# A hybrid encoder layer on one NeuronCore: first chunk pair of the feed-forward as plain products, operands in long-lived slots, second product's first loads moved

## The chip, the cores and the metric

The kernel runs on one core of one Trainium2 chip. The core has TensorE (matmuls into the accumulation memory, PSUM), VectorE, ScalarE and GpSimd (elementwise work on the on-chip memory, SBUF), and SyncE, whose queue issues the DMA transfers here. The engines run side by side, each through its own instructions in order, and wait for each other by semaphores. The metric is the device time of one execution in microseconds, as the median of several runs.

## The reference

One layer: two groups of attention heads side by side, a projection, and a gated feed-forward with a three-tap convolution along the tokens. There are 1024 tokens (and 16 learned meta tokens in front of them, which the output leaves out), 1024 model columns and 2816 hidden columns. Everything is float32.

```python
u = rmsnorm(h, norm_mix_pre)
o_na = rmsnorm(neighbourhood_attention(q_na, k_na, v_na, rpb), na_gain)   # 8 heads
o_gl = gla_bidirectional(q_gl, k_gl, v_gl, g_gl, z_gl, ...)               # 4 heads
mix = jnp.concatenate([o_na, o_gl], axis=-1) @ w_o
h = h + rmsnorm(mix, norm_mix_post)
a = rmsnorm(h, norm_ffn_pre) @ w_ffn_in
ap = jnp.pad(a, ((0, 0), (half, half), (0, 0)))
a = sum(ap[:, j:j + L] * conv_w[j] for j in range(CONV_W)) + conv_b
val, gate = a[..., :D_FF], a[..., D_FF:]
y = (jax.nn.gelu(gate, approximate=True) * val) @ w_ffn_out
return h + rmsnorm(y, norm_ffn_post)
```

## The kernel before

**Precision.** TensorE multiplies in a rounded float32 form (`fp32r`). To keep float32's accuracy each operand is split in two: ScalarE casts it to the rounded form (`hi`), VectorE subtracts that from the original (`lo`). A product of two operands is then three matmuls, hi x hi, hi x lo and lo x hi. So every operand costs one ScalarE and one VectorE pass before TensorE can use it.

**Upstream.** Projections, gated linear attention (GLA) and the meta tokens' part come first, then neighbourhood attention (NA), whose V windows are copied from DRAM to DRAM in layouts of their own (`vw_d`). The projection `W_o` is loaded in 8 blocks (`wor`), split into `woh` and `wol`, and applied to nine token units of 128 (`wo`, units 0 to 8; unit 8 is the last). Each unit then has two norms: `rsa` after `W_o`, and `rsb` ahead of the feed-forward. Of each norm the last step, a product of one column (L147), runs on GpSimd. The normed unit (`un`) is transposed by TensorE (`pt`, L836) and copied into `u2r`, the feed-forward's input with all 1024 tokens. Units 1 to 5 go by way of DRAM (`ut`). The lists `T2` and `T3` write out by hand in which order these steps are put into the program (`wg`: matmuls of a unit, `wn` and `wt`: its norms and transposes, `ul`: a unit read back, `u15`: one column copied, `fr`: the first weight loads).

**First product.** The hidden columns are worked off in 22 chunk pairs j, each of a value and a gate block of 128 columns. Tokens are taken in two halves, the 1024 input columns in two halves as well, so a pair is a product of 2 x 2 blocks, which the kernel does by seven block products in place of eight (`prod`, operations 1 to 7, the Strassen-Winograd scheme). It needs sums of the blocks: of the inputs `a11`, `a12`, `a21`, `a22` once (`a_sum`, VectorE, `as`), of the weights in each pair (`bt`, GpSimd, L920 to L923, from the raw weights `fr`), and of the results (`evac`, `c`) in each pair. The letters `q_r`, `q_x`, `q_z` are PSUM tiles of these products. One block product is 24 matmuls of 128x258 (2 token quarters, 4 blocks of 128 input columns, 3 terms), so a pair has 168. The convolution (`conv`: one ScalarE and two VectorE steps), the GELU and the gating give `y`, stored to `y_d`.

**Second product.** It is a seven-product scheme too, over pairs of chunk pairs. Its operands are y and the output weights themselves, sums of y (`s_sums`, GpSimd, to `s_d`) and sums of the weights (`t_sums`, GpSimd, from loads `w`, to `t_d`). The sums are made during the first product and go through DRAM. Then seven sweeps of 11 steps follow (`sweep`, `operands`): a step loads two raw operands (`ra`, `rb`), splits them, and does 12 matmuls of 128x512, 924 in all (L1111 to L1113). At the end each of 8 token units is finished by its norm and the residual (`hr`, loaded ahead).

**What sets the order.** A scheduler orders each engine's instructions when the program is built, from the order in which the code is written, some priorities, and the tiles' dependences. Tiles come from pools; a pool with n buffers under a tag hands them out in turn, and whoever takes one waits until its last user is done. On the SyncE queue a DMA that waits holds up the ones behind it. Before, the sums of the weights (`t_sums`) stand in even pairs and have a buffer `w` of their own, and the second product's pools open after the first product's have been closed.

## Time and profile before

| | us |
|---|---|
| runs of the kernel before | 1361.99, 1364.66, 1368.95 (median 1364.66) |
| profiled execution: its own time | 1369.85 |
| profiled execution: span of its instructions | 1368.1 |
| TensorE busy (matmuls) | 1266.1 (93%) |
| VectorE, ScalarE, GpSimd busy | 891.3 (65%), 620.8 (45%), 429.3 (31%) |
| DMA | 203.73 MB, 149 GB/s on average |

A row of the trace names an engine (PE is TensorE, PEld its weight loads, DVE VectorE, ACT ScalarE, POOL GpSimd, SP SyncE, SPq its DMA queue), the line of the kernel, the operation, and its tiles with the output before the arrow. Busy shares are averages over stages with different limits, so the trace is read by stretches. A waiting instruction is listed with what released it. Spans on GpSimd are rough.

### The profile page before, as it was taken

What the parts mean: (1) busy time and instruction counts of PE and PEld (TensorE: products, weight loads), DVE (VectorE), ACT (ScalarE), POOL (GpSimd) and SP (SyncE); (2) the same over time, 40 slices, a digit from 0 to 9 for tenths busy, and PEclk for the clock granted to TensorE, in tenths of its full rate; (3) what the DMA queues carried; (4) which work ended last, traced back from release to release, by engine and by line L of the source; (5) the groups of instructions that cost most, each with busy time, mean ns of one, the idle gap of its engine ahead of it and who ended that gap; (6) DMA issues with size and microseconds to landing.
All of it is one profiled execution on the core that took longest, in us unless ns stands there. A gap on an engine that the chain in (4) does not pass through costs nothing.

```text
span 1368.1 us, 23454 instructions
## 1 busy us (share of the span) xinstructions
PE 1266.1 (93%) x9024; PEld 1136.5 (83%) x9026; DVE 891.3 (65%) x1444; ACT 620.8 (45%) x1182; POOL 429.3 (31%) x402
## 2 busy tenths in 40 slices
PE   7979999999899899996799898999999985999997
PEld 6869888889778668775799898999999974888776
DVE  5481365455354657668898988878878853455557
ACT  5443544523244555555444343544444432445543
POOL 1170001000122326433667778555454311000001
PEclk9989999999999899997899999999999997999999
DMA  6311132112875974443256556332322218767734
GB/s 201 117 38 48 39 90 82 58 56 67 262 227 171 283 225 147 156 169 124 97 196 211 188 204 240 113 109 94 123 93 96 76 65 294 272 193 217 236 108 169
DMA packets 116432, 203.73 MB, mean 149 GB/s; under 512 B 17376, under 2 KB 50496, under 8 KB 116320
## 3 DMA queue, kind: packets, MB, share of 16 engines
q1 hardware_dynamic: 116320, 202.23, 44.6%
q8 instruction: 71, 1.16, 0.3%
q14 instruction: 41, 0.34, 0.1%
HBM read 145.64 MB, written 66.19 MB: 155 GB/s over the span
## 4 chain that ended last, share of the span: by engine, by line
PE 67%; DMA 12%; POOL 7%; DVE 6%; issue 4%; ACT 2%; SPq 1%; POOLq 0%; DVEq 0%; ACTq 0%
PE q_r L967 4%; PE q_r L968 4%; PE q_r L969 4%; PE r L1111 3%; PE r L1112 3%; PE r L1113 3%; DMA w<-in_w_ffn_out_dram 2%; PE pna L178 2%; DMA ra<-y_d 2%; PE pna L179 2%; PE pna L180 2%; PE q_z L968 2%; PE q_z L967 2%; PE q_z L969 2%; PE ops L690 2%
## 5 line engine op out<-in xcount | busy, mean ns | idle before, releaser
L967 PE MATMUL q_r<-ah,bh 128*128 128x258 f32 x704 | 202.7, 288 | 23.2 <-ACT c L1015 16.1
L968 PE MATMUL q_r<-al,bh 128*128 128x258 f32 x704 | 201.5, 286 | 1.0 <-DVE al L152 1.0
L969 PE MATMUL q_r<-ah,bl 128*128 128x258 f32 x704 | 198.7, 286 | 0.0
L967 PEld LDWEIGHTS q_r<-ah,bh 128*128 128x128 f32 x704 | 135.8, 193 | 25.5 <-ACT c L1015 17.1
L968 PEld LDWEIGHTS q_r<-al,bh 128*128 128x128 f32 x704 | 135.9, 193 | 1.3 <-DVE al L152 1.3
L969 PEld LDWEIGHTS q_r<-ah,bl 128*128 128x128 f32 x704 | 135.1, 193 | 0.0
L152 DVE TENSOR_TENSOR bl<-rb,bh 128x512 fp32r<-128x512 f32 x77 | 53.0, 690 | 79.1 <-ACT bh L151 73.0
L967 PE MATMUL q_z<-ah,bh 128*128 128x258 f32 x352 | 100.6, 286 | 3.3 <-DVE c L1065 3.2
L968 PE MATMUL q_z<-al,bh 128*128 128x258 f32 x352 | 100.4, 285 | 0.0
L969 PE MATMUL q_z<-ah,bl 128*128 128x258 f32 x352 | 99.9, 284 | 0.0
L908 DVE TENSOR_TENSOR bl<-bt,bh 128x512 fp32r<-128x512 f32 x88 | 85.0, 966 | 5.5 <-ACT bh L906 5.5
L151 ACT CAST bh<-rb 128x512 fp32r<-128x512 f32 x77 | 47.7, 622 | 87.4 <-PE r L1112 33.1
L1010 ACT ACTIVATE g<-g 128x512 f32<-128x512 f32 x44 | 27.8, 633 | 130.8 <-DVE g L1003 130.8
L920 POOL TENSOR_TENSOR bt<-fr,fr 128x512 f32<-128x512 f32 x22 | 47.7, 2167 | 117.9 <-DVE bl L908 54.7
L908 DVE TENSOR_TENSOR bl<-fr,bh 128x512 fp32r<-128x512 f32 x66 | 63.9, 970 | 24.3 <-ACT bh L906 24.1
L147 POOL TENSOR_TENSOR rsc_r<-rsc_v,nhalf 128x1 f32<-128x1 f32 x8 | 5.7, 715 | 222.2 <-DVE rsc_v L146 222.2
L1111 PE MATMUL r<-bh,ah 128*128 128x512 f32 x176 | 55.7, 396 | 20.4 <-ACT bh L151 20.4
L967 PEld LDWEIGHTS q_z<-ah,bh 128*128 128x128 f32 x352 | 67.2, 191 | 4.2 <-DVE c L1065 4.2
L1112 PE MATMUL r<-bh,al 128*128 128x512 f32 x176 | 68.3, 395 | 0.0
L1113 PE MATMUL r<-bl,ah 128*128 128x512 f32 x176 | 68.2, 395 | 0.0
L969 PEld LDWEIGHTS q_z<-ah,bl 128*128 128x128 f32 x352 | 67.3, 191 | 0.0
L968 PEld LDWEIGHTS q_z<-al,bh 128*128 128x128 f32 x352 | 67.1, 191 | 0.0
(355 smaller groups left out, 4011.4 us busy)
## 6 DMA issues: line engine op xcount, KB each, us to landing
fr<-in_w_ffn_in_dram SPq DMA_DIRECT2D x44, 512.0 KB
...
```

Of the source, the lines that this page charges most:

```text
L151: nc.scalar.copy(hi, src)
L152: nc.vector.tensor_tensor(lo, src, hi.bitcast(F32), ALU.subtract)
L178: mm(ps[:m, :n], wh, uh[:, k, t0 : t0 + n], start=(k == 0), stop=False)
L908: nc.vector.tensor_tensor(lo, src, hi.bitcast(F32), ALU.subtract)
L920: nc.gpsimd.tensor_sub(f[5], b12, b11)
L967: mm(ps[:, t, :258], hi[:, k, :], ah[:, k, c], start=(first and k == 0), stop=False, skip_group_check=True)
L968: mm(ps[:, t, :258], hi[:, k, :], al[:, k, c], start=False, stop=False, skip_group_check=True)
L969: mm(ps[:, t, :258], lo[:, k, :], ah[:, k, c], start=False, stop=(k == 3), skip_group_check=True)
L1010: nc.scalar.activation(g, g, AF.Gelu_apprx_tanh)
L1111: mm(ps, A[0][:, tk], B[0], start=first, stop=False, skip_group_check=True)
L1112: mm(ps, A[1][:, tk], B[0], start=False, stop=False, skip_group_check=True)
L1113: mm(ps, A[0][:, tk], B[1], start=False, stop=last, skip_group_check=True)
```

## The change

- **Input.** `u2r` becomes two tiles `u2a` and `u2b` of 514 columns, one for each token half with its overlap; the overlapping columns are copied by GpSimd. The copies out of PSUM move to ScalarE, except one of unit 8. Units 3 to 5 are read back into buffers of the weight ring `fr`, and `T3` has another order.
- **Pair 0.** It is done by eight plain block products (`plain_prods`), first both of the first token half, then those of the second, the last of them after unit 8's transposes. Its results are convolved in quarters (128x256). It needs no weight sums (`prep`), no result sums, and takes its PSUM from the pools of the stage before. Pairs 1 to 21 keep the seven products.
- **Operands.** The split inputs live in slots of two pools that stay open to the end: `mixp` ("m", where the GLA output was) and `wop` ("w0" to "w7", where the split `W_o` blocks were). Splits and sums of the inputs are made in two column parts. The pools release buffers tile by tile (`reuse_waits="tile"`).
- **Weight sums.** `t_sums` moves to odd pairs, ahead of `s_sums`, and its tiles share the ring "y" of 6 buffers with the gated outputs. Stores go by halves.
- **Second product.** The raw operands of the first sweep's first eight steps (`pre`) are loaded in the last pair into "m", "w4" and "w5". The raw ring has 6 buffers for both operands (before 8 + 8), the split ring 9 (before 3 of each kind), the splits of operation 4 lie in "m", "w0" to "w7" and 4 more buffers, the residual ring has 4 buffers (before 5), and the PSUM banks are assigned by number.

The first place is SyncE's queue while the last attention heads begin. `vw_d` are the copies of V windows, `wor` the raw `W_o` blocks, `kt` and `vt` operands of attention. Before:

```order
L553 DMA vt_0_2_4795<-vw_d_0_2_147 96x3x256
L727 DMA wor_5044<-in_w_o_dram 128x1024
L203 DMA v_d<-pvn_s_4751 128x256
L727 DMA wor_5050<-in_w_o_dram 128x1024
L553 DMA vt_0_3_4797<-vw_d_0_3_148 72x3x256
L849 DMA g_norm_mix_post<-in_norm_mix_post_dram 128x1024
L635 DMA kt_0_2_5099<-kT_d_58 128x576
L635 DMA kt_0_2_5101<-kT_d_59 128x576
L502 DMA vw_d_1_0_141<-v_d 264x1x256
```

After:

```order
L202 DMA v_d<-pvn_s_4751 128x256
L554 DMA vt_0_3_4797<-vw_d_0_3_148 72x3x256
L503 DMA vw_d_1_0_141<-v_d 264x1x256
L503 DMA vw_d_1_1_142<-v_d 352x1x256
L503 DMA vw_d_1_2_143<-v_d 352x1x256
L503 DMA vw_d_1_3_144<-v_d 264x1x256
L503 DMA vw_d_1_0_149<-v_d 192x1x256
L503 DMA vw_d_1_1_150<-v_d 256x1x256
L503 DMA vw_d_1_2_151<-v_d 256x1x256
L503 DMA vw_d_1_3_152<-v_d 192x1x256
L731 DMA wor_5044<-in_w_o_dram 128x1024
L731 DMA wor_5049<-in_w_o_dram 128x1024
```

The two `W_o` loads stood ahead of the window copies and now stand behind all eight.

The second place is the seam before the first product, on two engines. First TensorE, between the last `W_o` products (`wo`) and the first product of the feed-forward. `pt_7` and `pt_8` are transposes of units 7 and 8, `c_...` the plain products of pair 0, `q_r` a product of the seven. Before:

```order
L836 MATMUL pt_7_0_7032<-ident,un_7_6774 128x128 x4
L836 MATMUL pt_7_1_7038<-ident,un_7_6774 128x128 x4
L836 MATMUL pt_5_0_7046<-ident,ut_7044 128x128 x4
L836 MATMUL pt_5_1_7052<-ident,ut_7044 128x128 x4
L836 MATMUL pt_8_0_7099<-ident,un_8_6916 128x128 x4
L836 MATMUL pt_8_1_7105<-ident,un_8_6916 128x128 x4
L967 MATMUL q_r<-ah_7117,bh_1_7062 128x258
L967 MATMUL q_r<-ah_7117,bh_1_7192 128x258
L967 MATMUL q_x<-ah_7119,bh_2_7074 128x258
```

After:

```order
L764 MATMUL wo_1_1_7002<-wo_5081,mh_1_6982 128x512
L842 MATMUL pt_7_0_7061<-ident,un_7_6766 128x128 x4
L963 MATMUL c_0_7084<-a_7073,bh_11_7045 128x258
L964 MATMUL c_0_7084<-a_7073,bh_11_7045 128x258
L842 MATMUL pt_7_1_7067<-ident,un_7_6766 128x128 x4
L965 MATMUL c_0_7084<-a_7073,bl_11_7047 128x258
...
L965 MATMUL c_0_7217<-ah_7186,bl_22_7059 128x258
L842 MATMUL pt_8_0_7242<-ident,un_8_6908 128x128 x4
L842 MATMUL pt_8_1_7248<-ident,un_8_6908 128x128 x4
...
L965 MATMUL c_1_7283<-ah_7186,bl_22_7059 128x258
L963 MATMUL q_r<-a_7073,bh_1_7313 128x258
L964 MATMUL q_r<-a_7073,bh_1_7313 128x258
```

The first product no longer comes behind unit 8's transposes; the products of three of pair 0's four token quarters stand ahead of unit 8's, and pair 1 follows.

At the same place, GpSimd. `bt` are weight sums of a pair, `rsa_r` and `rsb_r` the last steps of the units' norms, the last of them those of unit 8. Before:

```order
L920 TENSOR_TENSOR bt_5_7196<-fr_1_7190,fr_0_7188 128x512
L921 TENSOR_TENSOR bt_6_7197<-fr_1_7190,bt_5_7196 128x512
L922 TENSOR_TENSOR bt_7_7198<-fr_1_7190 128x512
L810 TENSOR_TENSOR un_8_6916<-un_8_6916,g_norm_mix_post 128x512
L923 TENSOR_TENSOR bt_4_7199<-fr_0_7188,bt_6_7197 128x512
L147 TENSOR_TENSOR rsb_r<-rsb_v,nhalf 128x1
L147 TENSOR_TENSOR rsa_r<-rsa_v,nhalf 128x1
L147 TENSOR_TENSOR rsb_r<-rsb_v,nhalf 128x1
```

After:

```order
L938 TENSOR_TENSOR bt_5_7317<-fr_1_7311,fr_0_7309 128x512
L939 TENSOR_TENSOR bt_6_7318<-fr_1_7311,bt_5_7317 128x512
L940 TENSOR_TENSOR bt_7_7319<-fr_1_7311 128x512
L815 TENSOR_TENSOR un_8_6908<-un_8_6908,g_norm_mix_post 128x512
L941 TENSOR_TENSOR bt_4_7320<-fr_0_7309,bt_6_7318 128x512
L146 TENSOR_TENSOR rsa_r<-rsa_v,nhalf 128x1
L938 TENSOR_TENSOR bt_5_7580<-fr_1_7574,fr_0_7572 128x512
L939 TENSOR_TENSOR bt_6_7581<-fr_1_7574,bt_5_7580 128x512
L940 TENSOR_TENSOR bt_7_7582<-fr_1_7574 128x512
L146 TENSOR_TENSOR rsb_r<-rsb_v,nhalf 128x1
L941 TENSOR_TENSOR bt_4_7583<-fr_0_7572,bt_6_7581 128x512
```

Unit 8's `rsb_r` still stands behind the sums of two pairs; these are pairs 1 and 2, where they were 0 and 1.

The third place is SyncE's queue at the end of the first product. `ra`, `rb` and `r` are raw operands of the second. Before:

```order
L1040 DMA y_d_81<-y_12165 128x2x512
L1040 DMA y_d_82<-y_12414 128x2x512
L1040 DMA s_d_103<-y_12165 128x2x512
L1040 DMA s_d_104<-y_12414 128x2x512
L1100 DMA ra_0_12586<-y_d_61 128x512
L1100 DMA rb_0_12588<-in_w_ffn_out_dram 128x512
L1100 DMA ra_1_12610<-y_d_63 128x512
L1100 DMA rb_1_12612<-in_w_ffn_out_dram 128x512
```

After:

```order
L1119 DMA pre_12487<-y_d_61 128x512
L1120 DMA pre_12487<-in_w_ffn_out_dram 128x512
...
L1105 DMA y_d_81<-y_12248 128x512 x2
L1092 DMA t_d_115<-w_0_12657 128x2x512
L1092 DMA t_d_115<-w_1_12658 128x2x512
L1105 DMA y_d_82<-y_12508 128x512
L1105 DMA s_d_104<-y_12508 128x512
L1105 DMA y_d_82<-y_12508 128x512
L1105 DMA s_d_103<-y_12248 128x512 x2
L1105 DMA s_d_104<-y_12508 128x512
L1181 DMA r_8_12852<-y_d_77 128x512
L1181 DMA r_8_12852<-in_w_ffn_out_dram 128x512
```

The first eight steps' loads have gone ahead of the last pair's stores, and what stands behind these now is the ninth step's load, `r_8`.

The diff, cut to what the text speaks of:

```diff
 T3 = (
-    "wt 6", "wn 7", "u15", "ul 1", "ul 2", "wg 8", "ul 4", "wn 8", "ul 3", "wt 7", "ul 5", "fr",
+    "wt 6", "wn 7", "ul 1", "ul 2", "wg 8", "ul 3", "ul 4", "ul 5", "u15", "wn 8", "fr", "wt 7",
 )
...
+    wop = ctx.enter_context(tc.tile_pool(name="wop", reuse_waits="tile", bufs=1))
...
+    def quad(n, name, dt=F32R):
+        return wop.tile([P, 4, HC], dt, tag=f"w{n}", name=name)
...
-        raw = pp3.tile([P, D], F32, tag="xr", name=f"wor{k}", bufs=2)
+        raw = pp3.tile([P, D], F32, tag="ut", name=f"wor{k}", bufs=2)
...
+        plain = j == 0
...
+        if plain:
+            for op, b in (("11", b11), ("21", b21), ("12", b12), ("22", b22)):
+                b_split(j, op, b)
+            return
...
+    parts = (slice(0, 258), slice(258, HC))
...
+    def prods(ps, w, A, t, first, last):
+        c = slice(256 * t, 256 * t + 258)
+        for k in range(4):
+            mm(ps, w[0][:, k, :], A[0][:, k, c], start=(first and k == 0), stop=False, skip_group_check=True)
+            mm(ps, w[0][:, k, :], A[1][:, k, c], start=False, stop=False, skip_group_check=True)
+            mm(ps, w[1][:, k, :], A[0][:, k, c], start=False, stop=(last and k == 3), skip_group_check=True)
...
+    def plain_prods(half, t):
+        for c, bank in (("1", (ps_b, ps_a)), ("2", (ps_c, ps_s))):
+            ps = plain[half, c, t] = bank[half == 0](f"c{half}{c}_{t}")
+            for x, op in enumerate((1, 2) if half == 0 else (0, 4)):
+                prods(ps[:, :258], wts[0, f"{x + 1}{c}"], aops[op], t, x == 0, x == 1)
...
+    for t in range(2):
+        plain_prods(0, t)
...
+    plain_prods(1, 0)
     step2("wt 8")
+    a_split(0, a21, parts[1])
+    a_split(4, a22, parts[1])
+    plain_prods(1, 1)
...
+    prep(1)
...
+    def ring4(name):
+        return fc.tile([P, 4, 256], F32, tag="y", name=name, bufs=6)
...
-        w = fc.tile([P, 2, 2, 512], F32, tag="w", name=f"w{k}")
+        w = [ring4(f"w{k}_{c}").rearrange("p (h d) b -> p h (d b)", h=2) for c in range(2)]
...
+        if j == NFC - 1:
+            t = mixp.tile([P, 8, HC], F32, tag="m", name="pre1")
+            raws = [t[:, x, :512] for x in range(8)]
+            for w in (4, 5):
+                t = quad(w, f"pre{w}", F32)
+                raws += [t[:, x, :512] for x in range(4)]
+            for k in range(8):
+                pre.append(raws[2 * k : 2 * k + 2])
+                nc.sync.dma_start(pre[k][0], y_d[2 * k][0])
+                nc.sync.dma_start(pre[k][1], a["w_ffn_out"][2 * k][0])
...
         if j % 2:
+            t_sums(j // 2)
             s_sums(j // 2, ys[j - 1], y)
-        else:
-            t_sums(j // 2)
...
-            raws[x] = half(f"r{x}", f"r{x}{op}_{k}", 8)
-            nc.sync.dma_start(raws[x], src)
...
+        if op == 1 and k < len(pre):
+            raws = pre[k]
+        else:
+            raw = (fb if i % 2 else fo).tile([P, KC, P], F32, tag="fr", name=f"r{op}_{k}", bufs=3)
...
-        hrs[i] = fo.tile([P, D], F32, tag="hr", name=f"hr{i}", bufs=5)
+        hrs[i] = fo.tile([P, D], F32, tag="hr", name=f"hr{i}", bufs=4)
```

## Rows read from the trace of the kernel before

**Rows 1.** Stretches (microseconds), busy time and instructions of each engine, clock, DMA.

```profile
core 0: us, PE busy (x) PEld busy (x) DVE busy (x) ACT busy (x) POOL busy (x), PEclk, DMA share, GB/s
460.00:500.00 40.00, 38.48 (x326) 27.37 (x327) 23.26 (x70) 23.96 (x62) 10.73 (x20) 0.92 0.89 269
620.00:640.00 20.00, 11.85 (x58) 8.83 (x56) 16.33 (x25) 9.78 (x17) 9.10 (x8) 0.75 0.57 202
640.00:680.00 40.00, 27.79 (x192) 26.99 (x193) 35.76 (x25) 19.36 (x20) 22.07 (x8) 0.78 0.19 66
700.00:800.00 100.00, 92.68 (x742) 90.90 (x741) 89.26 (x91) 42.69 (x72) 73.98 (x48) 0.98 0.61 211
800.00:900.00 100.00, 93.23 (x750) 92.42 (x749) 83.73 (x90) 42.48 (x73) 66.71 (x43) 0.97 0.47 166
900.00:1000.00 100.00, 100.00 (x837) 100.00 (x837) 83.84 (x101) 47.68 (x80) 50.92 (x31) 1.00 0.31 111
1120.00:1130.00 10.00, 2.80 (x24) 2.58 (x22) 5.00 (x7) 2.68 (x4) 0.00 (x0) 0.74 0.13 52
1145.00:1160.00 15.00, 15.00 (x60) 12.20 (x59) 7.00 (x11) 6.53 (x11) 0.00 (x0) 0.87 1.03 381
1160.00:1280.00 120.00, 120.00 (x530) 98.98 (x529) 63.71 (x99) 59.10 (x108) 0.00 (x0) 1.00 0.72 233
```

**Rows 2.** TensorE's waits, 700 to 1110, then 1110 to 1368: total, times, longest.

```profile
PE q_r L967 <- ACT c L1015: 5.4, 3, 2.6
PE q_r L967 <- DVE y L1003: 5.0, 4, 2.6
...
PE r L1111 <- ACT bh L151: 20.4, 1, 20.4
```

**Rows 3.** Timeline, SyncE's queue and TensorE near 456: start, duration, operation [idle before].

```profile
456.38 9.56 SPq L502 DMA_DIRECT2D vw_d<-v_d  x8
457.59 0.79 PE L757 MATMUL wo<-woh,mh 128*128 128x512 f32 x1 [4.55 <-ACT woh L151]
```

**Rows 4.** Timeline at the first seam: TensorE, then VectorE, then GpSimd.

```profile
622.19 0.40 PE L759 MATMUL wo<-wol,mh 128*128 128x512 f32 x1
640.22 0.80 PE L967 MATMUL q_r<-ah,bh 128*128 128x258 f32 x2 [2.04 <-ACT ah L151]
639.01 2.30 DVE L981 TENSOR_TENSOR as<-u2r 128x2056 f32<-128x2056 f32 x1
661.32 4.50 DVE L152 TENSOR_TENSOR al<-as,ah 128x2056 fp32r<-128x2056 f32 x2
681.12 0.75 DVE L1002 SCALAR_TENSOR_TENSOR g<-c,vec,g 128x512 f32<-128x512 f32 x1 [0.88 <-ACT g L999]
655.32 11.64 POOL L920 TENSOR_TENSOR bt<-fr,fr 128x512 f32<-128x512 f32 x1 [20.54 <-DVE bl L908]
667.03 1.27 POOL L921 TENSOR_TENSOR bt<-fr,bt 128x512 f32<-128x512 f32 x1
```

**Rows 5.** Chain of waits: start, length, what, in three places.

```profile
783.40 6.04 DMA fr<-in_w_ffn_in_dram
...
1143.19 2.04 PE r L1111 x4
...
1292.03 4.33 DMA ra<-y_d
```

**Rows 6.** The page's groups: weight splits beside idle and beside busy GpSimd.

```profile
L152 DVE TENSOR_TENSOR bl<-rb,bh 128x512 fp32r<-128x512 f32 x77 | 53.0, 690 | 79.1 <-ACT bh L151 73.0
...
L908 DVE TENSOR_TENSOR bl<-bt,bh 128x512 fp32r<-128x512 f32 x88 | 85.0, 966 | 5.5 <-ACT bh L906 5.5
```

**Rows 7.** Timeline at the second product's start and end.

```profile
1130.45 1.26 POOL L1032 TENSOR_TENSOR y<-y,y 128x512 f32<-128x512 f32 x1 [27.24 <-issue]
1134.42 1.70 SPq L1040 DMA_DIRECT2D s_d<-y  x2
1360.81 0.39 PE L1113 MATMUL r<-bl,ah 128*128 128x512 f32 x1
```

More of the change, by code (lines that the diff above doesn't have):

```diff
@@ L61 @@
 BTOT = 12 * (24 + 32 + 24)
+HC = 2 * 256 + 2
 NLATE = 5
@@ L756, in wo_mm @@
                 kk = k if part else 4 + k
-                mm(ps, mh[:, k, :], woh[kk][:, cs], start=(k == 0), stop=False)
+                x = mm(ps, mh[:, k, :], woh[kk][:, cs], start=(k == 0), stop=False)
+                if i == 8 and hf == 0 and k == 0:
+                    tc.keep_in_program_order(x)
                 mm(ps, ml[:, k, :], woh[kk][:, cs], start=False, stop=False)
@@ new lines, in gated @@
+    def gated(j, name, src, val):
+        if len(val.shape) == 2:
+            g = mixp.tile([P, 256], F32, tag="ssq", name=f"g{j}_{name}", bufs=2)
+        else:
+            g = mixp.tile([P, 2, 256], F32, tag="mnb", name=f"g{j}_{name}", bufs=4)
+        conv(j, 1, src, g)
+        nc.scalar.activation(g, g, AF.Gelu_apprx_tanh)
+        nc.vector.tensor_mul(val, val, g)
+    y0 = [mixp.tile([P, 2, 256], F32, tag="mnb", name=f"y0_{x}", bufs=4) for x in range(2)]
+    for half in range(2):
+        for t in range(2):
+            val = y0[half][:, t]
+            conv(0, 0, plain[half, "1", t][:, :258], val)
+            gated(0, f"{half}{t}", plain[half, "2", t][:, :258], val)
@@ L954 @@
+    psum_s.close()
     ps1s = ExitStack()
[L955 removed]
+    ps1 = ps1s.enter_context(tc.tile_pool(name="ps1", reuse_waits="tile", bufs=1, space=bass.MemoryType.PSUM))
     acc1 = {}
[L958 to L969 removed]
@@ L989, with acc_tile @@
-    a_split(4, a22)
-    nc.vector.tensor_tensor(s2, a12, s2, ALU.subtract)
-    a_split(3, s2)
+    def acc_tile(j, key):
+        tag = f"r{j % 2}" if key == "r" else key
+        acc1[j, key] = ps1.tile([P, 2, 512], F32, tag=f"q{tag}", name=f"q{j}_{key}")
+    for j, key in ((1, "z"), (2, "r"), (1, "r"), (1, "x")):
+        acc_tile(j, key)
+    def prod(j, op, key, first):
+        if (j, key) not in acc1:
+            acc_tile(j, key)
+        for t in range(2):
+            prods(acc1[j, key][:, t, :258], wts[j, op], aops[op], t, first, True)
@@ new lines, with a_sum @@
+    prod(1, 1, "r", True)
+    prod(1, 2, "x", True)
+    def a_sum(dst, x, y, alu, c):
+        nc.vector.tensor_tensor(dst[:, :, c], x[:, :, c], y[:, :, c], alu)
+    for c in parts:
+        a_sum(a22, a21, a22, ALU.add, c)
+        a_sum(s2, a22, a11, ALU.subtract, c)
+        a_split(6, s2, c)
+    for c in parts:
+        a_split(5, a22, c)
+    for c in parts:
+        a_sum(a21, a11, a21, ALU.subtract, c)
+        a_split(7, a21, c)
+    ops_tiles(3, 6, 7)
+    for c in parts:
+        a_sum(s2, a12, s2, ALU.subtract, c)
+        a_split(3, s2, c)
@@ L1115 @@
     o4 = []
+    steps = []
+    late = []
     def sweep(op, ps, first):
@@ L1123, in sweep, with copies @@
                 o4.append(operands(4, len(o4)))
-    def copies(name, ps):
-        r = [half(name, f"{name}_{t}", 4) for t in range(4)]
+    def copies(dst, ps):
         for t in range(4):
-            nc.scalar.copy(r[t], ps[t])
-        return r
-    R = [ps2.tile([P, H], F32, tag="r", name=f"r{t}", bufs=4) for t in range(4)]
-    Z = [ps2.tile([P, H], F32, tag="z", name=f"z{t}", bufs=4) for t in range(4)]
+            nc.scalar.copy(dst[t], ps[t])
+    banks = [ps2.tile([P, H], F32, name=f"bank{t}") for t in range(8)]
+    R, Z = banks[2:4] + banks[6:], banks[:2] + banks[4:6]
     sweep(1, R, True)
-    c11 = copies("c11", R)
+    c11 = [half("c11", f"c11_{t}", 4) for t in range(4)]
+    copies(c11, R)
     sweep(2, Z, True)
@@ L1140 @@
     sweep(6, R, False)
-    c12 = copies("c12", R)
+    c12 = [half("c12", f"c12_{t}", 4) for t in range(4)]
+    copies(c12, R)
+    c22 = [half("c22", f"c22_{t}", 4) for t in range(4)]
     sweep(7, R, False)
-    c22 = copies("c22", R)
+    copies(c22, R)
+    t = mixp.tile([P, 8, HC], F32R, tag="m", name="late")
+    late += [t[:, x, :512] for x in range(8)]
+    for w in (0, 1, 2, 3, 4, 5, 6, 7):
+        t = quad(w, f"late{w}")
+        late += [t[:, x, :512] for x in range(4)]
+    late += [half("late", f"late{x}", 4, F32R) for x in range(4)]
     sums = fo.tile([P, 2 * 8], F32, name="sums")
```

205 lines of the change are left out of this document (101 added, 104 removed).

## The prediction

> **What bounds the kernel now.** I read the page first, then the table by stretches, then TensorE's waits, then the timelines at the seams. TensorE is busy in most stretches, and every other engine has room on average, so a time is saved only where TensorE stands. In [rows 1] the reader sees where. From 900 to 1000 us TensorE runs 837 matmuls of 258 columns in 100 us without a gap, 0.1195 us each; from 1160 to 1280 it runs 530 of 512 columns in 120 us, 0.2264 each. These two paces price all that follows.
>
> The first feed-forward product has 22 x 168 = 3696 matmuls, 441.7 us at that pace. It begins at 640.22 [rows 4] and its last 24 matmuls end 2.80 us after 1120 [rows 1], so it takes 482.6 us: 40.9 are lost. From 640 to 680 there are 192 matmuls (22.9 us' worth) in 40 us: 17.1 lost. From 700 to 900 there are 742 + 750 = 1492 (178.3) in 200 us: 21.7 lost, to waits for VectorE's and ScalarE's convolutions [rows 2] and a granted clock of 0.98 and 0.97, so that some of it ran at 1.2 GHz. That leaves 2.1. Between the products TensorE stands 20.4 us for the first operand of the second [rows 2]. The second product runs from 1143.19 [rows 5] to 1361.2 [rows 7], 218.0 us, where 924 x 0.2264 = 209.2 are needed. The span ends 6.9 later, at 1368.1. Ahead of it all, TensorE loses 20 - 11.85 = 8.2 us from 620 to 640 [rows 1], when the last token unit's norms are on their way.
>
> **Upstream: W_o loads behind the window copies.** Before, the first W_o loads are issued ahead of eight copies of V windows, whose issue takes 9.56 us, and TensorE still waits 4.55 us for the first weights [rows 3]. After, the copies come first. The copies issue earlier too, since nothing of W_o is ahead of the store they wait for, and TensorE has attention work to put in the gap. So the cost lies between 0 (the earlier issue makes up for all) and 10 (the whole issue time, to the next microsecond); a gain is excluded, since no load moves forward. I take the middle, **+5**. The row shows 269 GB/s from 460 to 500 [rows 1], and the eight copies move 2128 KB, 8.1 us at that rate. The Trainium skill, "DMA: Bandwidth & Descriptors", section "Queues, rings and completion order", says that each DMA engine takes a queue's descriptors in ring order; by that alone the loads would lose those 8.1 us, and the sum would be 3 us longer.
>
> **First seam.** The change lets chunk pair 0 begin on the first token half. Its eight products have 192 matmuls in place of 168: 24 x 0.1195 = +2.9 us of TensorE. In return TensorE has 192 + 48 = 240 matmuls (28.7 us' worth: all of pair 0, and two products of pair 1) to do while VectorE makes the other operands, and VectorE is the bound there. Its order after the last W_o product (622.6, [rows 4]) holds, up to the last operand part that pair 1's third and fourth products need: 20 splits and sums of half width at 1.15 (half of the 2.30 row), 7 weight splits at 0.69 [rows 6], 16 quarter convolutions at about 0.42 and 4 gates at 0.4 (estimates from the 0.75 row of twice the width), and the last unit's own steps, about 5.6 (seven of 0.7 to 1.3, by the same rows). That is 23.0 + 4.8 + 6.7 + 1.6 + 5.6 = 41.7 us: 664.3.
>
> To it come waits. The last unit's second norm runs through GpSimd, and in the new order its small product stands behind the weight sums of pairs 1 and 2. Those of pair 2 want a weight block whose buffer is free only after pair 1's sums: five GpSimd steps of about 1.5, a load of 6.04 [rows 5], three more steps. From about 627, when pair 1's second block can be there (its buffer is free after pair 0's first splits, at about 621, and the load takes 6.04), this gives 627 + 7.5 + 6.0 + 4.5 = 645, against 637.5 at which VectorE (14.7 us of the above) reaches the step that waits: some 8 us. Stretching of VectorE beside GpSimd adds the rest; a weight split takes 966 ns in the first product and 690 in the second, where GpSimd rests [rows 6]. Low end: 664.3 + 8.2, the idle time of 620 to 640, = 672.5. High end: 41.7 x 966/690 = 58.4, plus 8.2, = 689.2. I take **679**, nearer the low end because GpSimd is busy in part of that time only.
>
> **Pacing.** 3720 - 240 = 3480 matmuls remain at 679: 415.9 us, to 1094.9. Before, GpSimd is busy 73.98 and 66.71 of 100 us from 700 to 900, running weight sums ahead, and 50.92 from 900 to 1000, where TensorE never waits [rows 1]. Paced, the 16 GpSimd steps of each two pairs at 50.92/31 = 1.64 take 26.2 of 40.1 us, 65%: near the row of 800 to 900 in load, but without its convolution lag from the seam. I leave 3 us of waits (bounds 0 and 21.7): the first product ends at **1097.9**, 24.9 earlier.
>
> **Second seam.** The first eight steps' operands are loaded during the last pair into slots that are dead by then, so the 20.4 us go. TensorE does not stop, so the slow start goes too: 4 + 60 matmuls took 1160 - 1143.2 = 16.8 us, at a granted clock of 0.87 in the last 15 [rows 1], where 14.5 are needed: 2.3. What is late next is the ninth step's operand, whose load stands in SyncE's queue behind the last sums' stores. Before, these are issued at 1134.42 for 1.70 us, 13.3 after the product's end; with a load of 4.33 [rows 5] and a split it is there at about +19, wanted after 8 x 12 x 0.2264 = 21.7. But GpSimd's four sums took 1.26 each beside an idle VectorE [rows 7]; at 1.74 they end 2 later, and y may be late by as much. I take **+2** (0 to 5). The shallower residual ring ties the last residual loads to earlier finishes: **+1** (0 to 4.33, a load). The shallower raw ring I hold at no cost; the fourth rival is the case in which it costs.
>
> **Sum.** 1097.9 + 5 + (218.0 - 2.3 + 2) + 6.9 + 1 = 1328.5 against the span of 1368.1: -39.6. The profiled execution took 1369.85, 1.75 beyond its span, and is the longest of about the same as the three runs (median 1364.66). Taken from the median: **1325**.
>
> **Rivals.**
> *Gains in full.* Upstream 0, 672.5 at the seam, no waits left, no late operand, no tail: 5 + 6.5 + 3 + 2 + 1 = 17.5 less, 1307.5. For it: each low end has a row. Against: all at once.
>
> *GpSimd starved at the first seam.* One GpSimd sum shows 11.64 us from 655.32, while VectorE runs long two-input operations back to back, where the next, beside little, takes 1.27 [rows 4]. If that happens to the sums ahead of the last unit's norm, VectorE reaches the waiting step and stands for most of the eight steps, some 10 us: 1335. Against: halves of 1.15 leave more openings than the 4.50 pairs of before. The Trainium skill, "SBUF — State Buffer", section "Who interferes with whom", states the rule that speaks against this change: a VectorE operation with two SBUF inputs and a GpSimd operation that reads SBUF exclude each other, and the second to start is blocked. The 11.64 row agrees with it.
>
> *Raw ring too shallow.* Two sweeps issue 33 operand loads in 22 steps of 2.72 us (59.8 us) over six buffers: a buffer must come round within 10.9. With a load of 4.33, the split and the queue at 14 (an estimate), the sweeps take 33 x 14/6 = 77: +17, 1342. Against: 233 GB/s in the steady part leave room [rows 1].
>
> *Seam and pacing gain nothing.* If VectorE (89.26 of 100 us busy from 700) is the bound and the lag merely moves, the 24.9 stay: 1350.
>
> *Slower: GpSimd paces the first product.* The weight sums now share six buffers with the gated outputs, so a late sum stalls the convolutions and then TensorE. With 16 steps in 40.1 us this begins at a mean step of 2.51 us; at 2.78 it eats the whole gain. At 2.9 it costs (46.4 - 40.1) x 10 = 63: 1388. Against: 1.64 in the row of 900 to 1000 and 73.98/48 = 1.54 in that of 700 to 800. For: the 11.64 row.
>
> **Chances.** Forecast 0.44; gains in full 0.12; starved GpSimd 0.15; raw ring 0.12; no gain in seam and pacing 0.10; slower 0.07. The range of 1305 to 1352 leaves out the last and some of the edges. A measurement of this kernel tells about 0.5%, 6.8 us, from no change. Faster by more: all but the slower case and the part (0.05) of the fifth case in which upstream is dear as well and a load is late: 0.87. Within: 0.05. Slower: 0.08.
>
> **What would show it.** The first W_o product some 5 us later than 457.59; pair 0's first matmul before the last unit's transposes, pair 1's third product at about 684 (with upstream); 837 matmuls per 100 us from there on; no wait over 5 us between the products; the second product in about 218 us. A GpSimd row of over 5 us at the first seam, waits for raw operands in the second product, or convolutions that wait for a buffer of stores would prove me wrong, each for its rival.

## The result: 0.6% faster, a fifth of what was forecast

The changed kernel takes 1356.62 us (median of 10 runs, 1352.45 to 1361.46) against 1364.78 (10 runs) of the kernel before: ratio 0.9938, 95% interval 0.9918 to 0.9959. That is faster, by 8 us where 40 were forecast, and the time lies above the range; the interval reaches to both sides of the 0.5% that the prediction set as its bound. The profiled execution took 1360.31 us with a span of 1358.6, 9.5 less than the span before.

The table by stretches of the changed kernel, with the columns of [rows 1]:

```profile
460.00:500.00 40.00, 32.24 (x261) 24.01 (x259) 19.32 (x57) 18.77 (x49) 9.24 (x19) 0.66 0.97 289
620.00:640.00 20.00, 17.67 (x96) 13.99 (x94) 8.90 (x17) 11.28 (x24) 4.04 (x6) 1.00 0.27 96
640.00:660.00 20.00, 18.88 (x136) 17.68 (x137) 17.85 (x19) 14.44 (x26) 11.30 (x8) 1.00 0.43 141
660.00:680.00 20.00, 11.22 (x71) 9.98 (x70) 19.50 (x28) 10.73 (x16) 5.27 (x4) 0.78 0.10 40
680.00:700.00 20.00, 12.51 (x92) 12.04 (x90) 19.22 (x23) 9.09 (x14) 7.88 (x1) 0.84 0.23 70
700.00:800.00 100.00, 97.06 (x788) 96.69 (x788) 84.95 (x89) 42.73 (x72) 63.27 (x40) 0.97 0.40 141
800.00:900.00 100.00, 97.06 (x805) 96.46 (x804) 89.06 (x98) 45.72 (x78) 58.09 (x37) 1.00 0.41 146
900.00:1000.00 100.00, 95.79 (x792) 95.01 (x792) 89.76 (x94) 43.99 (x75) 62.43 (x39) 1.00 0.46 161
...
1160.00:1280.00 120.00, 120.00 (x531) 99.39 (x530) 65.72 (x103) 61.26 (x112) 0.00 (x0) 1.00 0.70 234
```

Read it against [rows 1] in four places. From 460 to 500 TensorE is busy 32.24 in place of 38.48, at a granted clock of 0.66 in place of 0.92. From 660 to 700 VectorE is busy 38.72 of 40 us while TensorE has 23.73. From 700 on no stretch is poor any more, but none is full: 788, 805 and 792 matmuls, where 742, 750 and 837 stood. The second product's pace is as it was.

TensorE's timeline of the changed kernel at four places: the first `W_o` product, the last of the unbroken run of these products, the third and fourth products of chunk pair 1, and the first matmul of the second product (start, duration, operation, idle time before and its releaser). Below it stand two matmuls of the kernel before, which the table needs.

```profile
473.65 0.80 PE L760 MATMUL wo<-wo,mh 128*128 128x512 f32 x1 [5.68 <-ACT wo L150]
...
629.62 0.39 PE L764 MATMUL wo<-wo,mh 128*128 128x512 f32 x1
...
696.11 0.55 PE L963 MATMUL q_z<-ah,bh 128*128 128x258 f32 x1 [5.23 <-DVE y L1012]
...
700.63 0.58 PE L963 MATMUL q_r<-ah,bh 128*128 128x258 f32 x1 [2.89 <-ACT c L1076]
...
1137.81 0.39 PE L1197 MATMUL bank<-oh,oh 128*128 128x512 f32 x1
```
```profile
612.04 0.40 PE L758 MATMUL wo<-woh,ml 128*128 128x512 f32 x1
...
683.64 0.28 PE L968 MATMUL q_z<-al,bh 128*128 128x258 f32 x1
```

The first product ends at 1137.8, the second starts in the same microsecond and ends at 1351.6. The spans split like this. In the last column the upstream term is measured at the `W_o` matmul with 36 of them still to come, 612.04 before and 629.62 after (there the unbroken run ends). The seam is from that one to the matmul with which 3474 of the first product's are left, 683.64 before and 700.63 after: the first one behind the last wait of the seam.

| part | forecast | measured |
|---|---|---|
| upstream, to the end of the `W_o` run | +5 | +17.6 |
| first seam | -4 | -0.6 |
| rest of the first product | -21 | -2.0 |
| between the products | -20.4 | -20.4 |
| second product and tail | +0.7 | -4.1 |
| span | -39.6 | -9.5 |

One of five terms holds to the microsecond. Upstream costs more than three times its 5 us, and of the 25 us that the first seam and the rest of the first product were to give, 2.6 came. The experiments take these three first.

### The profile page after: what moved, and what is told of

Its sections match the earlier page's. It is cut to its first block, busy times and chain, and to the rows that moved or that the text cites. A ratio compares the mean times of both kernels' runs of the same rounds, so it can differ in the third digit from the quotient of the medians.

```text
span 1358.6 us, 23572 instructions
## 1 busy us (share of the span) xinstructions
PE 1272.8 (94%) x9048; PEld 1142.4 (84%) x9050; DVE 910.7 (67%) x1453; ACT 620.3 (46%) x1198; POOL 430.2 (32%) x401
## 4 chain that ended last, share of the span: by engine, by line
PE 66%; DVE 18%; DMA 6%; issue 4%; ACT 4%; SPq 1%; POOL 0%; DVEq 0%; ACTq 0%; POOLq 0%
DVE bl L921 5%; PE bank L1198 4%; PE bank L1197 4%; PE bank L1199 4%; PE q_r L963 3%; PE q_r L964 3%; PE q_r L965 3%; PE ops L691 2%; PE wo L760 2%; PE wo L764 2%; PE wo L763 2%; PE pna L177 2%; PE pna L178 2%; PE pna L179 2%; PE q_z L963 2%
## 5 line engine op out<-in xcount | busy, mean ns | idle before, releaser
L963 PE MATMUL q_r<-ah,bh 128*128 128x258 f32 x504 | 144.3, 286 | 12.4 <-ACT c L1076 12.4
L964 PE MATMUL q_r<-al,bh 128*128 128x258 f32 x504 | 143.3, 284 | 0.0
L965 PE MATMUL q_r<-ah,bl 128*128 128x258 f32 x504 | 143.0, 284 | 0.0
L151 DVE TENSOR_TENSOR ol<-r,oh 128x512 fp32r<-128x512 f32 x116 | 74.5, 687 | 46.9 <-ACT oh L150 46.6
L1197 PE MATMUL bank<-oh,oh 128*128 128x512 f32 x264 | 102.9, 390 | 2.9 <-DVE c L1263 2.9
L1198 PE MATMUL bank<-oh,ol 128*128 128x512 f32 x264 | 102.7, 389 | 0.0
L1199 PE MATMUL bank<-ol,oh 128*128 128x512 f32 x264 | 102.2, 389 | 0.0
L150 ACT CAST oh<-r 128x512 fp32r<-128x512 f32 x116 | 65.6, 619 | 50.3 <-PE bank L1198 40.8
L921 DVE TENSOR_TENSOR bl<-fr,bh 128x512 fp32r<-128x512 f32 x67 | 67.2, 1007 | 17.8 <-ACT bh L919 17.6
L177 PE MATMUL pna<-uh,wna_h 128*128 128x272 f32 (+2 forms) x192 | 64.2, 335 | 4.8 <-DVE qsl L151 4.8
L178 PE MATMUL pna<-ul,wna_h 128*128 128x272 f32 (+2 forms) x192 | 65.0, 339 | 0.0
```

The lines of the kernel that those rows point to most:

```text
L150: nc.scalar.copy(hi, src)
L151: nc.vector.tensor_tensor(lo, src, hi.bitcast(F32), ALU.subtract)
L177: mm(ps[:m, :n], wh, uh[:, k, t0 : t0 + n], start=(k == 0), stop=False)
L178: mm(ps[:m, :n], wh, ul[:, k, t0 : t0 + n], start=False, stop=False)
L921: nc.vector.tensor_tensor(lo, src, hi.bitcast(F32), ALU.subtract)
L963: mm(ps, w[0][:, k, :], A[0][:, k, c], start=(first and k == 0), stop=False, skip_group_check=True)
```

## Upstream: the W_o loads

SyncE's queue (start, time that the issue took, operation), in the kernel before and then in the changed one:

```profile
448.08 0.49 SPq L727 DMA_DIRECT2D wor<-in_w_o_dram  x1
448.66 0.52 SPq L203 DMA_DIRECT2D v_d<-pvn_s  x1
449.54 0.33 SPq L727 DMA_DIRECT2D wor<-in_w_o_dram  x1
```
```profile
451.16 0.58 SPq L202 DMA_DIRECT2D v_d<-pvn_s  x1
...
457.18 7.66 SPq L503 DMA_DIRECT2D vw_d<-v_d  x8
464.88 1.95 SPq L731 DMA_DIRECT2D wor<-in_w_o_dram  x2
```

The copies did not issue earlier than the 456.38 of [rows 3]; the loads issue some 16 us later than before, when two had gone out by 449.54. The granted clock (the first number behind the engines) fell in both kernels; before, from 440 to 480:

```profile
440.00:460.00 20.00, 13.86 (x132) 10.96 (x131) 9.85 (x37) 7.49 (x19) 4.08 (x10) 0.81 0.82 230
460.00:480.00 20.00, 19.56 (x172) 15.39 (x173) 13.33 (x46) 13.06 (x37) 7.14 (x13) 0.85 0.91 294
```

After:

```profile
440.00:460.00 20.00, 18.27 (x210) 15.60 (x209) 11.91 (x51) 9.53 (x29) 5.20 (x11) 0.99 0.61 181
460.00:480.00 20.00, 14.32 (x101) 10.51 (x100) 5.98 (x14) 6.71 (x16) 2.24 (x5) 0.50 0.89 286
```

So part of what 460 to 500 shows had its counterpart before 460 in the kernel before: from 440 to 500 the clock is 0.89 there and 0.77 after. `e1_wo_first` puts the loads ahead of the copies again, by their priority alone.

```diff
-        nc.sync.dma_start(raw, a["w_o"][:, k, :])
+        with tc.high_priority(offset=1000):
+            nc.sync.dma_start(raw, a["w_o"][:, k, :])
```

> The changed kernel with one thing undone: the loads of the raw W_o blocks go ahead of the eight V window copies again. Theory (the upstream term was sized too small): the first W_o product, at 473.6 us in the changed kernel and at 457.6 before the change, comes at about 463, the granted clock from 460 to 500 rises from 0.66 to about 0.9, and the time falls by 10 to 16 us, to about 1343. Rival (the late W_o loads are made up for by attention work that TensorE does meanwhile, and the loss lies at the first seam): the first W_o product moves but the time falls by 4 us at most.

Measured: 1347.37 us, ratio 0.9875 (0.9824 to 0.9925), 9 below the changed kernel. Its first `W_o` product starts at 460.4, its `W_o` run ends at 612.9, and its stretch has the clock and the work of before:

```profile
460.00:500.00 40.00, 38.05 (x308) 27.35 (x309) 25.85 (x73) 25.75 (x64) 9.63 (x20) 0.92 0.97 300
```

So the order of these loads costs about 9 us of median time. With four runs of `e1` this is rough: its interval and that of the changed kernel just touch. It is a little under the theory's 10 to 16 and over the rival's 4. In profiles of kernels that keep the order (`e2`, `e3`, `e4`, `e7`, `e8` below) the `W_o` run ends between 621.4 and 627.0, in `e1`, `e6` and `e10` between 612.9 and 617.7; the 629.6 of the changed kernel is the long end, and the +17.6 of the table holds some of such scatter.

## The first product: the weight sums

Four kernels take the sums apart. `e2_no_wsums` leaves the 44 GpSimd subtractions of the weights out, with their loads and stores kept; the instruction order on TensorE, VectorE and ScalarE is unchanged.

```diff
-        nc.gpsimd.tensor_sub(b11, b12, b11)
-        nc.gpsimd.tensor_sub(b12, b22, b12)
-        nc.gpsimd.tensor_sub(b22, b22, b11)
-        nc.gpsimd.tensor_sub(b21, b21, b22)
```

> The changed kernel without the arithmetic of the second product's weight sums on GpSimd (44 instructions; loads and stores stay, so t_d holds the raw weights and the output is not the layer's). The order on TensorE, VectorE and ScalarE is the same. Theory (GpSimd's sums slow VectorE wherever they stand, so pacing spread the loss and did not remove it): TensorE's waits from 700 to 1110, 14.8 us in the changed kernel, fall under 3, a weight split on VectorE falls from about 1.04 to under 1.0 us, and the time falls by 15 to 20 us, to about 1339. Rival (VectorE's own work in the new order is the bound, GpSimd or not): waits stay over 10 us and the time falls by less than 5.

`e3_wsums_even` undoes the pacing alone: the sums in even pairs, with a buffer of their own.

```diff
-        return fc.tile([P, 4, 256], F32, tag="y", name=name, bufs=6)
+        return fc.tile([P, 4, 256], F32, tag="y", name=name, bufs=4)
...
+        wb = fc.tile([P, 2, 2, 512], F32, tag="w", name=f"w{k}")
+        w = [wb[:, c] for c in range(2)]
...
+    t_sums(0)
...
-            t_sums(j // 2)
...
+        else:
+            t_sums(j // 2)
```

> The changed kernel with the pacing undone: weight sums in the even pairs again, in a buffer of their own, and four buffers for the gated outputs; TensorE, VectorE and ScalarE keep their order. Theory (the loss to GpSimd's sums is the same wherever they stand): the waits gather between 700 and 900 and none is left after it, and the time is that of the changed kernel within 4 us, 1353 to 1361. Rival (pacing is worth what the prediction gave it, and something else holds up the first product): the time rises by 12 to 18 us, to about 1371.

`e10_wsums_dve` is `e1_wo_first` with the same sums on VectorE, in the same places.

```diff
-        nc.gpsimd.tensor_sub(b11, b12, b11)
+        nc.vector.tensor_sub(b11, b12, b11)
...
```

> e1_wo_first with the 44 weight sums of the first product done by VectorE, in the same places, in place of GpSimd. In the changed kernel VectorE is busy 353.1 of the 387.9 us that TensorE is busy in 700 to 1100 (0.911), and without the sums 333.8 of 400 (0.834): GpSimd's sums cost VectorE 0.077 x 418 = 32 us of stretched instructions. On VectorE itself 44 sums at the 690 ns of an undisturbed 128x512 subtraction take 30 us. Theory (what counts is VectorE's total, and a GpSimd sum costs it about what VectorE would need to do the sum itself): nothing gained, 1343 to 1351, with waits of TensorE for q_r and y as before. Rival (it is the single long hold of 1.7 us by a GpSimd sum that makes TensorE wait, while short sums slip between): the first product is nearly free, 1332 to 1339.

Measured: `e2` 1337.96 us, ratio 0.9806 (0.9778 to 0.9834); `e3` 1362.95, ratio 0.998 (0.9957 to 1.0003); `e10` 1348.25, ratio 0.9863 (0.9833 to 0.9892), the same as `e1`. The stretch of 700 to 1100 in the changed kernel, then `e2`, then `e10`, and for `e3` its two halves:

```profile
700.00:1100.00 400.00, 387.85 (x3191) 385.65 (x3192) 353.14 (x373) 176.57 (x301) 248.16 (x152) 0.99 0.42 149
```
```profile
700.00:1100.00 400.00, 400.00 (x3337) 400.00 (x3336) 333.78 (x390) 189.99 (x317) 185.93 (x114) 1.00 0.44 154
```
```profile
700.00:1100.00 400.00, 389.76 (x3201) 385.26 (x3200) 364.31 (x416) 177.70 (x302) 183.89 (x111) 1.00 0.42 148
```
```profile
700.00:900.00 200.00, 185.12 (x1480) 182.58 (x1479) 173.15 (x173) 83.15 (x140) 145.09 (x93) 0.97 0.56 200
900.00:1100.00 200.00, 200.00 (x1670) 200.00 (x1669) 170.53 (x199) 95.43 (x159) 96.75 (x60) 1.00 0.30 104
```

Without the sums' arithmetic 146 more matmuls fit into the 400 us, 17.4 us at 0.1195, though all their transfers stay; the median falls by 18.7, of which some is upstream scatter (the `W_o` run of `e2` ends at 624.7). Ahead of time (`e3`) the loss is gathered in 700 to 900; paced, it is spread over the whole product. Pacing is worth 6 us of median time (the theory allowed 4, the rival wanted 12 to 18; the two intervals just touch), and 5.9 in the profiles, from 3474 matmuls left to the product's end: 443.1 in `e3`, 437.2 in the changed kernel. Some 16 us stay, by 421.3 in `e2`. The kernel before took 439.2 there, so that against it only 2.0 of the 5.9 are left; what makes `e3` 4 us longer than the kernel before was not looked for. What VectorE waits for in 700 to 1100 says why: first in the changed kernel, then in `e2` (total, times, longest).

```profile
DVE bl L921 <- ACT bh L919: 18.3, 21, 2.6
DVE g L1011 <- ACT g L1008: 15.3, 18, 0.9
DVE y L1023 <- ACT g L1022: 12.6, 18, 0.7
```
```profile
DVE g L1011 <- ACT g L1008: 16.5, 19, 0.9
DVE c L1122 <- PE q_x L965: 15.6, 8, 2.0
```

In the changed kernel VectorE's 353.1 busy us and 46.2 us of waits for ScalarE fill the 400: it never waits for TensorE, so it is the bound, though its busy share reads 88%. ScalarE is not the bound in its place, although TensorE's longest waits name its copies `c`: it is busy 176.6 us of the 400 and itself waits for VectorE, in one line alone for 134.6.

```profile
PE q_r L963 <- ACT c L1076: 11.0, 8, 2.9
```
```profile
ACT g L1022 <- DVE g L1012: 134.6, 37, 7.6
```

In `e2` VectorE waits 15.6 us for TensorE's results, which is its spare time. `e10` says that the engine hardly matters: 44 sums on VectorE (0.68 us in the median, 33 us in all) cost TensorE what 44 of about 1.65 us on GpSimd cost. GpSimd's were paid by VectorE in longer instructions: 0.911 us for each us that TensorE was busy, in place of 0.834, which is 32 us over the product.

## The sums moved upstream

If VectorE has no time in the first product, the sums could go beside the gated linear attention, where it is busy about half the time. Three kernels, all on top of `e1`, move them there. `e5_wsums_up` puts a group of four on GpSimd behind each step:

```diff
+            w = gp.tile([P, 2, 2, 512], F32, tag="tw", name=f"w{k}_{h}", bufs=1)
...
+            nc.gpsimd.tensor_sub(b11, b12, b11)
...
+        if i < 11:
+            t_sums(i)
...
-            t_sums(j // 2)
```

> The kernel with the W_o loads ahead of the window copies, and with the second product's weight sums moved out of the first product: they are made beside GLA, where GpSimd is busy under 10% and the DMA engines under 30% of the time, through one 8 KB buffer. Theory (GpSimd's sums cost only where VectorE is nearly full): TensorE's waits from 700 to 1090 fall under 3 us as without the sums, the stages up to 440 us do not grow by more than 3, and the time is that of the kernel with the W_o loads first less 15 to 18, about 1330. Rival (the 22 MB of early transfers hold up the loads that the projections wait for, or GpSimd the gates): what is won later is lost before 440, and the time stays within 5 us of 1347.

`e9_wsums_late` keeps them behind GpSimd's gate steps (the edit against `e5`):

```diff
-            nc.gpsimd.tensor_sub(b11, b12, b11)
+            tc.keep_in_program_order(nc.gpsimd.tensor_sub(b11, b12, b11))
...
-        if i < 11:
-            t_sums(i)
+        for _ in range(SUMS[i]):
+            t_sums(nsum)
+            nsum += 1
```

> The changed kernel with the first W_o loads ahead (as in e1_wo_first) and GpSimd's 44 weight sums beside the gated linear attention (as in e5_wsums_up), but with the first of each group of four kept behind the program's earlier GpSimd work, so that none of them stands ahead of the last gate step; the groups are written two at a time between the later steps. Theory (the sums cost TensorE their 18 us only where VectorE is what TensorE waits for, and what e5_wsums_up lost upstream, its W_o stage starting at 471.5 instead of 460.4, came from gate steps queued behind sums on GpSimd's in-order queue, not from the ports or the 45 MB of extra traffic): the first W_o matmul starts at 458 to 464, the first product shows 100 us busy in every 100 us, and the time is 1327 to 1336. Rival (the loss upstream is contention: VectorE slowed by sums, or the loads and stores in the way of the attention's own transfers): the W_o stage still starts at 468 to 476 and the time stays at 1337 to 1347.

`e11_wsums_dve_up` gives them to VectorE there, with loads a step ahead:

```diff
+        tc.keep_in_program_order(nc.vector.tensor_sub(b11, b12, b11))
+        nc.vector.tensor_sub(b12, b22, b12)
...
+        if i < 11:
+            t_load(i)
+        if i >= 1 and i < 12:
+            t_sums(i - 1)
```

> e1_wo_first with the 44 weight sums done by VectorE beside the gated linear attention (a group of four behind each step, loads a step ahead), GpSimd doing none. Theory (a GpSimd sum holds up short VectorE instructions for its whole length, which is what e9_wsums_late lost upstream: its scan steps took up to 1380 ns instead of 352; VectorE itself is busy only about half the time there and does a sum in 0.7 us): scan steps stay at 352 ns, the W_o stage begins at 458 to 468, the first product shows 100 us in every 100, and the time is 1327 to 1337. Rival (upstream it is the 45 MB of loads and stores, in the way of the attention's own transfers, or any addition to VectorE, whose scans are the path there): the W_o stage begins at 472 or later and the time is 1341 or more.

Measured: `e5` 1341.39 us, ratio 0.9837 (0.9791 to 0.9883); `e9` 1361.7, ratio 0.9964 (0.9947 to 0.998); `e11` 1353.09, ratio 0.9896 (0.9853 to 0.9939). In all three TensorE is busy 100 us of each 100 from 800 on, as the theory said, but the first `W_o` product starts at 471.5, 495.6 and 475.2, in place of 460.4 in `e1`. Upstream is not free. `e9` was to begin at 458 to 464 by its theory and at 468 to 476 by its rival; its 495.6 and its time fit neither, and the theory that `e5` lost its time to gate steps queued behind sums finds no support here. `e9` shows the price of one sum most plainly: a stretch of GpSimd's timeline, then one of VectorE's in the same place.

```profile
228.48 1.29 POOL L539 TENSOR_TENSOR w<-w 128x512 f32<-128x512 f32 x1 [6.87 <-DMA w<-in_w_ffn_out_dram]
229.85 1.29 POOL L540 TENSOR_TENSOR w<-w 128x512 f32<-128x512 f32 x1
231.23 1.29 POOL L541 TENSOR_TENSOR w<-w 128x512 f32<-128x512 f32 x1
```
```profile
228.56 1.36 DVE L398 SCALAR_TENSOR_TENSOR gs<-gs,dec 64x128 f32<-64x128 f32 x1
...
230.29 1.01 DVE L402 SCALAR_TENSOR_TENSOR gs<-gs,dec 64x128 f32<-64x128 f32 x1
...
231.33 1.33 DVE L398 SCALAR_TENSOR_TENSOR gs<-gs,dec 64x128 f32<-64x128 f32 x1
```

A scan step with a median of 344 ns, issued 0.08 us behind the sum that starts at 228.48, ends 0.15 us behind that sum, after 1.36. In `e9` 19 of the 120 scan steps take over 0.5 us, 16.9 us more in all; the granted clock is lower too (0.88 from 200 to 250 and 0.86 from 300 to 350, where `e1` has 1.00), and how the 35 us that `e9` loses upstream divide was not separated. Where GpSimd does no sums (`e11`) all scan steps are short, of line 402 (351 to 354 ns) as of line 398 (count, and shortest, median and longest in ns):

```profile
L398 DVE SCALAR_TENSOR_TENSOR gs<-gs,dec x60: 325/343/346, 176.0 to 332.7; 64x128 f32<-64x128 f32 x60
```

For `e11` the rival was right all the same: it has no stretched scan and still loses 15 us upstream. VectorE waits there for transfers, which the loads and stores of the sums (23 MB, not the 45 of the expectation) share the queue with. From 0 to 480 us, first in `e11`, then in `e1`:

```profile
DVE qsl L151 <- DMA qr<-qT_d: 13.0, 1, 13.0
...
DVE qsl L151 <- DMA kT_d<-qst: 7.6, 1, 7.6
```
```profile
DVE qsl L151 <- DMA qr<-qT_d: 4.3, 1, 4.3
DVE qsl L151 <- DMA kT_d<-qst: 3.5, 1, 3.5
```

These two waits are 12.8 us longer than in `e1`. How the loss divides between these transfers and VectorE's own 31 us more was not separated. `e5` beats both kernels, by 1.6% and 1.1%; of its 6 us below `e1` the intervals do not tell.

## The first seam

Three kernels. `e6_wn8_first` is `e1` with the last unit's second half ahead of the other units' transposes:

```diff
-    "wt 6", "wn 7", "ul 1", "ul 2", "wg 8", "ul 3", "ul 4", "ul 5", "u15", "wn 8", "fr", "wt 7",
+    "wt 6", "wn 7", "ul 1", "ul 2", "wg 8", "wn 8", "ul 3", "ul 4", "ul 5", "u15", "fr", "wt 7",
```

> The kernel with the W_o loads ahead of the window copies, and the last token unit's second W_o half put ahead of the transposes of units 3 to 5. Theory (VectorE is the bound from the first splits to the last operand of pair 1, and the last unit's norm is off that path until its own transposes): the wait for the last unit's transposes (5.2 us) goes, the wait ahead of pair 1 stays or grows, and the time changes by less than 3 us. Rival (the late W_o half is what delays the seam): the time falls by 6 to 10 us, to about 1339.

`e7_no_taps0` is the changed kernel without VectorE's 16 quarter convolutions of chunk pair 0, `e8_no_bt12` without GpSimd's weight sums `bt` of pairs 1 and 2:

```diff
+        if j == 0:
+            return
```
```diff
+        if j > 2:
...
+        else:
+            f = {5: b11, 6: b22, 7: b12, 4: b21}
```

> The changed kernel without VectorE's 16 quarter taps of pair 0's convolution (0.47 us each, 7.5 in all), which leaves two of three taps out of pair 0's hidden columns. Theory (VectorE is the bound at the first seam): the first products of pair 1 that wait for the last operands, at 696 to 701 us in the changed kernel, come 6 to 8 us earlier against the end of the W_o products, and the time falls by 5 to 8, to about 1350. Rival (the seam hangs on ScalarE's casts or on the last unit's norm): less than 3 us.

> The changed kernel without the 8 GpSimd sums of weights of pairs 1 and 2, which stand in GpSimd's queue around the last unit's norms; raw weights take their place, so these two pairs' results are not the layer's. TensorE keeps its order. Theory (GpSimd slows VectorE's two-input operations at the seam, and its own sums hold nothing up): VectorE's splits of 1032 columns take 1.2 us each in place of up to 2.2, the seam is 4 to 7 us shorter, and the time falls by as much, to about 1351. Rival of the prediction (the last unit's norm starves behind the sums): the seam is 10 us or more shorter. Second rival (neither): less than 2 us.

Measured: `e6` 1346.82 us, ratio 0.9865 (0.9827 to 0.9904), as `e1`; `e7` 1346.36, ratio 0.9857 (0.982 to 0.9895); `e8` 1353.92, ratio 0.9904 (0.9875 to 0.9933). The times of `e7` and `e8` hold upstream scatter as well (their `W_o` runs end at 622.2 and 627.0), so the seam is read from there to the matmul with which 3432 of the first product's are left. In the changed kernel this is the first one behind pair 1's third and fourth products, 78.2 us behind the end of the `W_o` run; then come `e7` and `e8`.

```profile
707.83 0.28 PE L963 MATMUL q_r<-a,bh 128*128 128x258 f32 x1
```
```profile
688.98 0.39 PE L963 MATMUL q_r<-ah,bh 128*128 128x258 f32 x1 [2.90 <-ACT c L1078]
```
```profile
698.46 0.28 PE L966 MATMUL q_r<-a,bh 128*128 128x258 f32 x1
```

It is 66.8 in `e7`, where the two products come in another order, and 71.4 in `e8`; in the eight other kernels whose seam was left alone it lies between 75.1 and 78.7. Taking 7.5 us of work from VectorE (16 x 0.47) gives 11.4, more than the 6 to 8 expected, and taking GpSimd's sums away gives 6.8, of the 4 to 7 expected; moving TensorE's work (`e6`, 76.8 where `e1` has 77.7) gives nothing: one wait goes and 4.9 us for `al` come in its place. So VectorE sets this seam, and GpSimd lengthens it. By the end of the product 2.4 of the 11.4 and 3.8 of the 6.8 are lost again. VectorE's rows of the changed kernel show the second part:

```profile
640.81 1.23 DVE L151 TENSOR_TENSOR al<-u2a,ah 128x1032 fp32r<-128x1032 f32 x1
...
648.69 2.06 DVE L151 TENSOR_TENSOR a<-u2a,a 128x1024 fp32r<-128x1024 f32 x1 [0.18 <-ACT a L150]
...
655.95 2.21 DVE L151 TENSOR_TENSOR al<-u2b,ah 128x1032 fp32r<-128x1032 f32 x1
```

The same split takes 1.23 or 2.2. On GpSimd (idle time and its releaser in brackets):

```profile
667.57 0.55 POOL L146 TENSOR_TENSOR rsb_r<-rsb_v,nhalf 128x1 f32<-128x1 f32 x1 [1.62 <-DVE rsb_v L145]
683.33 7.88 POOL L941 TENSOR_TENSOR bt<-fr,bt 128x512 f32<-128x512 f32 x1 [15.21 <-DVE bl L921]
```

The last unit's norm step came as soon as VectorE had its input; it stood behind no sum. The long GpSimd row of [rows 4] is back (7.88), but it is a sum for pair 2, and the waits at 696.11 and 700.63 name VectorE and ScalarE.

## The second seam

`e4_no_pre` is the changed kernel without the early loads: the condition under which they are issued never holds.

```diff
-        if j == NFC - 1:
+        if j == NFC:
```

> The changed kernel without the early loads of the second product's first eight steps: these go through the raw ring, behind the last stores. Theory (the second seam gave what the prediction said): TensorE stands about 20 us between the products again and starts the second at the lower clock, so the time rises by 20 to 24 us, to about 1378. Rival (most of the seam's gain came from elsewhere, such as the bank numbers or the shared rings): it rises by 10 us or less.

Measured: 1373.35 us, ratio 1.0063 (1.0042 to 1.0084), 17 above the changed kernel, with one wait between the products:

```profile
PE bank L1197 <- ACT oh L150: 14.8, 1, 14.8
```

It answers to the 20.4 us in [rows 2]; the second product then takes 216.1 us in place of 213.8. The 17 us lie between the theory's 20 to 24 and the rival's 10. So the early loads are worth 17 us where the rest of the change is in place, and without them the changed kernel would be slower than the one before.

## Why the prediction was wrong

**Upstream (+5).** The step that failed is "the copies issue earlier too, since nothing of W_o is ahead of the store they wait for". In the changed kernel's trace the store comes at 451.16 in place of 448.66, and the copies at 457.18 in place of 456.38. The upper bound of 10 counted only the copies' issue time; the loads' own delay was 16 us, and TensorE's granted clock stood at 0.50 from 460 to 480, for which the sum had no term. The price is some 9 us by `e1`, 17.6 in the one profile. The 8.1 us that the Trainium skill's ring order ("DMA: Bandwidth & Descriptors", "Queues, rings and completion order") gave is nearer to `e1` than my 5.

**First seam (-4).** That VectorE sets the end was right (`e6`, `e7`), and so was the rejection of the starved-GpSimd rival (the 667.57 row). The size was nearly right too: 679 with the 17.6 us from upstream is 696.6, the third product begins at 696.11, and only the fourth waits on, until 700.63. But that is in part luck. The wait of some 8 us for the last unit's norm did not come: from 649 to 700 VectorE is never idle for more than 0.8 us. In its place splits took 2.06 to 2.21 beside GpSimd in place of 1.23, a stretch of 1.7 to 1.8 for some of them.

**Pacing (-18.7, of the -21).** This is the term that sank the forecast, with 19 of the 30 us that it was off. The step that failed is "near the row of 800 to 900 in load, but without its convolution lag from the seam. I leave 3 us of waits": the last 3474 matmuls took 437.2 us, 22 over their 415.1 at full pace. I read the row from 900 to 1000 (GpSimd 50.92, TensorE 100) as a level that a paced GpSimd could rise above, and priced GpSimd by its own room: 65% of 40.1 us. But that row stands where no weight sums are left, and the sums are paid by VectorE, which had the 89.26 in [rows 1]. What fitted was the rival "seam and pacing gain nothing", "if VectorE is the bound and the lag merely moves": I gave it 0.10, for 24.9 us, and pacing was worth 6 (`e3`). The Trainium skill's exclusion rule ("SBUF — State Buffer", "Who interferes with whom"), which I set against the seam alone, bears on the sums of the first product as well; the rows of `e9` agree with it, 1.36 us for a step of 0.34.

**Second seam (-20.4), tail (+1), raw ring.** The main term was right. TensorE does not stop, the second product takes 213.8 us where 217.7 were put down, and TensorE's only waits in it are 2.9 us for its last results, so neither late sums nor six raw buffers cost anything. The +2 for a late operand and the +1 for the tail did not come (the tail is 7.0 us, before 6.9). **Slower by GpSimd** did not come: a mean GpSimd step of 1.63 us from 700 to 1100 stayed below the 2.51 at which it was to begin.

The sign was right, with 0.87 for faster by over 0.5%, but it hangs on the second seam alone: without its early loads the change is slower (`e4`). The range ended at 1352 because the case in which the 24.9 us stay was put at 1350, with upstream at +5; the same case with upstream dear as well and a load late had a chance of 0.05 and no time of its own, and the measured 1356.62 is nearest to it.
